# Eight blocks of the second layer's modulation move from the first layer's output projection into the scan's plan

## The chip, the cores and the metric

The kernel runs on one core of one Trainium2 chip. The metric is the device time of one execution in microseconds (us). Engines are named as in the profile: PE (TensorE, with PEld for its weight loads), DVE (VectorE), ACT (ScalarE), POOL (GpSimd) and SP (SyncE, which here mostly issues DMAs).

## The reference

Two layers work on 512 latent tokens and 256 context tokens of width 1024. The first layer's mixer is a gated MLP with spatial mixing, the second's a bidirectional RWKV-7 scan; each is followed by a mixture of experts. Every layer is modulated by vectors made from the conditioning:

```python
for i in range(DEPTH):
    mod_l = silu_c @ ada_w[i] + ada_b[i]
    mod_c = silu_cc @ ada_w[i] + ada_b[i]
    sh1, sc1, gt1, sh2, sc2, gt2 = jnp.split(mod_l[:, None, :], N_MOD, axis=-1)
    csh1, csc1, cgt1, csh2, csc2, cgt2 = jnp.split(mod_c, N_MOD, axis=-1)
    hl = rmsnorm(x, norm1_g[i]) * (1 + sc1) + sh1
    ...                                   # mixer of the layer, on hl and hc
    x = x + gt1 * yl
    hl2 = rmsnorm(x, norm2_g[i]) * (1 + sc2) + sh2
    ...                                   # experts on hl2
    x = x + gt2 * hier_moe(...)
```

`ada_w[i]` is 1024 x 6144 floats, 24 MB a layer. The second layer's mixer needs only the first third of its product (`sh1`, `sc1`); `gt1` is wanted after the scan, and the rest by the experts behind it.

## The kernel before

**Modulation.** The 6144 columns of a layer are made in 12 blocks of 512. `ada_block` loads a block's 2 MB of weights in four DMAs of 512 KB into the ring `w_raw`, and `ada_product` multiplies: eight matmuls with the conditioning as the stationary operand (128 x 32, in four column tiles of the array, so that four partial sums stand in four groups of partitions), a copy of the 128 x 512 result to `ada_part` by ACT, four small matmuls with `sel` that add the groups and turn the row into columns (the "turn"), and an addition of the bias by DVE into `k.mod[l]`. Product and turn share one PSUM buffer (tag `ada`, one deep).

**Where the blocks stand.** The first layer's blocks are spread over the first layer's mixer (`phase_a`): 0 to 3 ahead of it, 4 to 7 and 8 to 11 between its two projections' column groups. The second layer's twelve stand in the output projection at the end of `phase_a`: for each half `n` of the columns a loop over `kb` takes two rows of weights (`load_split`, split into a high and a low part) and makes 36 matmuls of 512 columns; in rounds 0 to 5 of each half a block is made with it. `moe.load_early` then issues the first expert weights.

**The scan's plan.** After the first layer's experts, `Rwkv.run` projects and then runs the scan (`wkv`). The scan's order is made by a planner (`Plan`): every step has an engine, an assumed cost, its reads and writes, and a tag; buffers come from rings of fixed depth (`RINGS`). `Plan.run` takes, again and again, the step that can start first by these costs, and among the steps of its engine that could start within `WINDOW` (0.05 us) the one whose tag number plus `DUE` is lowest:

```python
t0, s0 = min(best, key=lambda x: x[0])
t, s = min((x for x in best if x[1].eng == s0.eng and x[0] <= t0 + WINDOW), key=lambda x: x[1].tag[1] + DUE[x[1].tag[0]][x[1].tag[2]])
```

The steps: `value` (the value projection, 48 PE steps of six matmuls, tag 0, due +8), `prep` of group m (attention within a chunk, tag 2m, due -3 or -5), `invert` of group m (tag 2m, due -0.5; a chain of 62 DVE operations with transposes and two pairs of PE products), and `scan` step h (tag h, due 0). There are six groups of four chunks (two directions, two chunks each). `late` releases the memory of the value projection and makes the state `S` and the buffers of the second set; it reads all stores of `value`, and all steps with such a buffer come behind it. `Plan.fill` puts filler matmuls (L1061) ahead of a PE step that is the first user of a PSUM bank: at least one for the rings `p` and `y`, more where the plan sees PE idle for over 0.3 us. `p` has three banks. `QY` holds a chunk's masked products from `prep` until the scan step of that chunk has read them. The instructions are then ordered once more by the compiler.

Of the kernel before, what the change touches and what calls it, by code (L numbers as in the profile page):

```python
# [9 lines left out]
F32 = mybir.dt.float32  # L10
# [3 lines left out]
ALU = mybir.AluOpType  # L14
# [3 lines left out]
P = 128  # L18
# [84 lines left out]
def ada_block(k, pool, ps, l, n, bufs=4, tag="ada", psbufs=1):  # L103

    ws = []
    for h in range(4):
        w = pool.tile([P, 2, 512], F32, name="w_raw", tag="w_raw", bufs=bufs)
        k.nc.sync.dma_start(w, ada_rows(k, l, n, 2 * h, 2))
        ws += [w[:, i, :] for i in range(2)]
    ada_product(k, ps, pool.tile([P, 512], F32, name="ada_part", bufs=1), l, n, ws, tag, psbufs)  # L110


def ada_rows(k, l, n, j, m):
# [4 lines left out]
def ada_product(k, ps, part, l, n, ws, tag="ada", bufs=1):  # L118
    nc = k.nc
    q = ps.tile([P, 512], F32, name="ada_ps", tag=tag, bufs=bufs)  # L120
    for j, w in enumerate(ws):
        g = j % 4
        nc.tensor.matmul(q[32 * g:32 * g + 32, :], k.cstat[:, j, :], w, start=(j < 4), stop=(j >= 4),  # L123
                         tile_position=(0, 32 * g))
    nc.scalar.copy(part, q)
    q2 = ps.tile([P, 8], F32, name="ada_ps2", tag=tag, bufs=bufs)
    for j in range(4):
        nc.tensor.matmul(q2[:, 2 * j:2 * j + 2], part[:, j * P:(j + 1) * P], k.sel, start=True, stop=True)
    b = k.pk("adab")[:, l * 48 + 4 * n:l * 48 + 4 * n + 4]
    nc.vector.tensor_tensor(k.mod[l][:, 4 * n:4 * n + 4, :], q2.rearrange("p (j s) -> p j s", s=2),  # L130
                            b[:, :, None].to_broadcast([P, 4, 2]), op=ALU.add)


def mod(k, l, which, s):
# [46 lines left out]
def phase_a(k, moe):  # L181
    nc, tc = k.nc, k.tc
    a = k.a
    with ExitStack() as es:
# [12 lines left out]
        rms_stats(k, sm, v[:, 2, D:], rstd, range(NT), "r1")  # L197
        for n in range(4):
            ada_block(k, wp, ps, 0, n)
        G1 = gains(k, sm, 0, 1, k.pk("n1g")[:, 0:8], "G1")  # L200

        def emit_h(j, ql, qc):
# [36 lines left out]
        with tc.tile_pool(name="a_u", bufs=1) as up:  # L239
            for n in range(4):  # L240
# [13 lines left out]
                for i in range(4):  # L254
# [15 lines left out]
                    for hf in range(2):  # L270
# [7 lines left out]
                        nc.vector.tensor_tensor(v[:, 3 * hf:3 * hf + 3, g * P:(g + 1) * P], t1,  # L278
                                                u.rearrange("p (c q) -> p c q", c=3), op=ALU.mult)
                ada_block(k, wp, ps, 0, 8 + n)  # L280
        es_h.close()
        k.G2 = {0: gains(k, k.consts, 0, 4, k.pk("n2g")[:, 0:8], "G20")}

# [11 lines left out]
        for n in range(2):  # L295
            cs = slice(n * 512, (n + 1) * 512)
            acc = [ps.tile([P, 512], F32, name="o_ps", tag="mm") for t in range(NT)]
            for kb in range(KW // 2):
                ws = load_split(k, wp, a["ga_w_out"][kb * 256:(kb + 1) * 256, cs], 2)
                if kb < 6:  # L300
                    ada_block(k, wp, ps, 1, 6 * n + kb)
                gs = []
                for j in range(2):
                    g = 2 * kb + j
                    gh = og.tile([P, NT, P], F32R, name="gh", bufs=3)
                    gl = og.tile([P, NT, P], F32R, name="gl", bufs=3)
                    split(k, gh, gl, v[:, :, g * P:(g + 1) * P])
                    gs.append((gh, gl))

                for t, j in by_tile(NT, range(2), kb == KW // 2 - 1):  # L310
                    mm3(k, acc[t], (gs[j][0][:, t, :], gs[j][1][:, t, :]), ws[j], kb + j == 0, 2 * kb + j == KW - 1)
            for t in range(NT):
                tmp = og.tile([P, 512], F32, name="o_tmp", bufs=3)
                nc.vector.tensor_tensor(tmp, acc[t], gtB[t // NTL][:, cs], op=ALU.mult)
                nc.vector.tensor_tensor(k.x[:, t, cs], k.x[:, t, cs], tmp, op=ALU.add)
                moe.squares(og, t, n)
        moe.load_early()


# [4 lines left out]
class Moe:  # L324
# [570 lines left out]
    def overflow(self, ep, ps, after):  # L895
# [5 lines left out]
        with tc.For_i(0, nv) as i:  # L901
# [57 lines left out]
            for g in after.groups:  # L959
# [14 lines left out]
NCL = NL // C  # L974
DECAY = -0.6065306597126334
RINGS = dict(p=3, s3=2, sn=1, y=2, cum=1, kk=1, T=1, r=1, BK=1, set0=4, set1=4, X=1, Lp=1, Dn=1, subt=2, subp=2, SV0=1, SV1=1, rhs=1,
             yt=1, y0=1, E30=1, E31=1, fin=1, QY=8, v=4, vraw=2, vhi=4, vlo=4, vst=4)
SAME = dict(PE=0.1, DVE=0.13, ACT=0.15, POOL=0.1, SP=0.1)
WINDOW = 0.05
ON = dict(dec="POOL", q0="DVE", q1="DVE", r="POOL", neg="ACT", f1="POOL", f2="POOL", f3="DVE", f4="DVE")  # L980
COST = dict(DVE=0.6, POOL=1.32, ACT=0.48)
DUE = dict(prep=(-3.0, -3.0, -5.0, -5.0), invert=(-0.5, -0.5), scan=(0.0, 0.0), finish=(0.5,), value=(8.0,), late=(-9.0,))
PINNED = ()
DMALAT = 1.8
LAT = dict(PE=0.2, DVE=0.1, ACT=0.1, POOL=0.2, SP=0.2)
# [129 lines left out]
class Rwkv:  # L1115
# [6 lines left out]
    def run(self, moe):  # L1122
        k = self.k
        tc = k.tc
        k.G2[1] = gains(k, k.consts, 1, 4, k.pk("n2g")[:, 8:16], "G21")
        with ExitStack() as es:
            dr = es.enter_context(tc.tile_pool(name="c_dram", bufs=1, space=bass.MemoryType.DRAM))
            self.dr = dr
# [344 lines left out]
    def wkv(self, moe):  # L1473
# [4 lines left out]
        with ExitStack() as es:  # L1478
# [34 lines left out]
            prep(0, 0, 1, 2, 3)  # L1513
            self.invert(0)
            prep(1, 0, 1)
            for m in range(G):
                if m + 1 < G:
                    prep(m + 1, 2, 3)
                    self.invert(m + 1)
                for z in range(2):  # L1520
                    self.scan_step(2 * m, z, order[z][2 * m])
                if m + 2 < G:
                    prep(m + 2, 0, 1)
                for z in range(2):
                    self.scan_step(2 * m + 1, z, order[z][2 * m + 1])
            pl.run(tc)
            self.ps["y"].release()
            self.sp.release()
            self.out(moe)

    def values(self, vp):

# [637 lines left out]
```

## Time and profile before

| | us |
|---|---|
| median of 3 runs (lowest, highest) | 2725.82 (2725.16, 2739.96) |
| the profiled execution | 2729.52 |
| its span, from first to last instruction | 2727.3 |
| PE busy / DVE busy / ACT busy / POOL busy | 2430.3 / 1126.4 / 747.9 / 419.0 |
| mean granted clock of TensorE | 0.935 of full |

In the rows, `out<-in` names the tiles, `x` a count, and a bracket at a line's end is the idle time before the instruction and what ended it. A float32 matmul is recorded as two instructions; a busy PE is not a PE at its peak.

### The profile page before, as it was taken

The numbers are of one execution on the slowest core, as the hardware profiler recorded it, in microseconds if no ns is written. First come the engines' busy times: TensorE is split into PE (matmuls) and PEld (weight loads), VectorE is DVE, ScalarE is ACT, GpSimd is POOL, SyncE is SP. The second block draws the span as 40 slices with busy tenths as digits, with TensorE's granted clock in tenths as the row PEclk, the third lists the DMA queues.
The fourth block names the chain that finished last, engine by engine and source line by source line (L and its number), as shares of the span: only waits on it lengthen the run. The fifth ranks groups of instructions, "written<-read, shape, count | busy, mean of one in ns | idle before, by whom it ended". The sixth has DMA issues, their size and how long they took to land. (4 is left out here: it accounts for less than half of the span.)

```text
span 2727.3 us, 39031 instructions
## 1 busy us (share of the span) xinstructions
PE 2430.3 (89%) x15492; PEld 1533.4 (56%) x15492; DVE 1126.4 (41%) x2000; ACT 747.9 (27%) x1265; POOL 419.0 (15%) x339
## 2 busy tenths in 40 slices
PE   6999999976999999968979899889888599998994
PEld 2778996753443333336745488788777443333331
DVE  3335333374131111158654364887787611111113
ACT  3222123331000000026554346566543110000001
POOL 0000000033333322220012111112222301000001
PEclk8999999987999999988978699899989799999997
DMA  7136227565899999942245564434246569999994
GB/s 241 55 123 211 83 93 238 184 244 190 316 402 422 420 398 412 405 184 71 98 144 176 148 178 120 103 90 107 68 118 214 203 258 413 419 419 415 417 415 176
DMA packets 280943, 640.26 MB, mean 235 GB/s; under 512 B 131948, under 2 KB 157804, under 8 KB 230325
## 3 DMA queue, kind: packets, MB, share of 16 engines
q1 hardware_dynamic: 266548, 608.69, 60.9%
q0 software_dynamic: 12768, 23.78, 2.4%
q10 hardware_dynamic: 1440, 5.24, 0.5%
q8 instruction: 124, 2.03, 0.3%
q14 instruction: 63, 0.51, 0.1%
HBM read 582.22 MB, written 77.59 MB: 242 GB/s over the span
## 5 line engine op out<-in xcount | busy, mean ns | idle before, releaser
L827 PE MATMUL gu_ps<-e_raw,xT 128*64 128x512 f32 (+1 forms) x2048 | 629.7, 597 | 15.0 <-DMA e_raw<-moe_w_up 11.9
L827 PEld LDWEIGHTS gu_ps<-e_raw,xT 128*64 128x64 f32 (+1 forms) x2048 | 227.4, 154 | 388.0 <-issue 335.8
L845 PE MATMUL o_ps<-e_raw,hT 128*64 128x512 f32 (+1 forms) x1024 | 317.9, 601 | 5.0 <-ACT hT L792 5.0
L892 DVE TENSOR_TENSOR h_e<-gu_ps,h_e 128x512 f32<-128x512 f32 x42 | 29.1, 692 | 512.2 <-PE gu_ps L827 512.2
L845 PEld LDWEIGHTS o_ps<-e_raw,hT 128*64 128x64 f32 (+1 forms) x1024 | 114.5, 153 | 168.7 <-issue 150.2
L891 ACT ACTIVATE h_e<-gu_ps 128x512 f32<-128x512 f32 x42 | 25.1, 597 | 550.2 <-PE gu_ps L827 546.9
L1061 PE MATMUL p<-ident 128*128 128x128 f32 x892 | 140.4, 301 | 9.6 <-ACT BKt L1746 5.2
L1061 PEld LDWEIGHTS p<-ident 128*128 128x128 f32 x892 | 118.5, 204 | 22.2 <-ACT BKt L1746 7.2
L756 POOL DMA_INDIRECT ybuf<-yo,idx x40 | 40.0, 1001 | 472.3 <-DVE yo L848 403.3
L792 ACT COPY xT<-eT_ps 128x512 f32<-128x512 f32 x42 | 24.6, 585 | 321.0 <-PE gu_ps L827 205.5
L848 DVE SCALAR_TENSOR_TENSOR yo<-o_ps,wslot,gt_e 128x512 f32<-128x512 f32 x44 | 33.0, 750 | 184.8 <-issue 132.6
L749 POOL DMA_INDIRECT xg<-hbuf,idx x42 | 43.9, 1045 | 347.6 <-PE eT_ps L791 333.7
L73 PE MATMUL u_ps<-hh,w_hi 128*128 128x384 f32 x256 | 89.9, 351 | 5.0 <-ACT w_hi L66 5.0
L848 DVE SCALAR_TENSOR_TENSOR yo<-o_ps,wslot,gt2B 128x512 f32<-128x512 f32 x40 | 29.9, 750 | 155.0 <-PE o_ps L845 153.5
L74 PE MATMUL u_ps<-hl,w_hi 128*128 128x384 f32 x256 | 87.0, 340 | 0.0
L75 PE MATMUL u_ps<-hh,w_lo 128*128 128x384 f32 x256 | 85.9, 340 | 0.9 <-DVE w_lo L67 0.9
L67 DVE TENSOR_TENSOR w_lo<-w_raw,w_hi 128x1024 fp32r<-128x1024 f32 x56 | 67.9, 1222 | 38.4 <-ACT w_hi L66 37.9
L123 PE MATMUL ada_ps<-w_raw,cstat 128*32 128x512 f32 x384 | 64.0, 636 | 21.4 <-DMA w_raw<-ada_w 20.8
L73 PE MATMUL v_ps<-w_hi,hh 128*128 128x512 f32 x192 | 74.8, 402 | 4.2 <-ACT w_hi L66 4.2
L1776 DVE TENSOR_TENSOR X<-X,subt 128x31 f32<-128x31 f32 (+15 forms) x186 | 75.8, 408 | 5.0
L74 PE MATMUL o_ps<-w_lo,gh 128*128 128x512 f32 x192 | 76.1, 396 | 0.0
L73 PE MATMUL o_ps<-w_hi,gh 128*128 128x512 f32 x192 | 75.8, 398 | 0.0
(526 smaller groups left out, 4505.0 us busy)
## 6 DMA issues: line engine op xcount, KB each, us to landing
e_raw<-moe_w_gate SPq DMA_DIRECT2D x128, 1024.0 KB, 20.0
e_raw<-moe_w_up SPq DMA_DIRECT2D x128, 1024.0 KB, 20.2
e_raw<-moe_w_down SPq DMA_DIRECT2D x128, 1024.0 KB, 20.1
w_raw<-ada_w SPq DMA_DIRECT2D x96, 512.0 KB, 5.6
w_raw<-ga_w_in SPq DMA_DIRECT2D x32, 512.0 KB, 4.2
Td<-c_st SPq DMA_DIRECT2D x64, 192.0 KB, 3.3
T<-Td SPq DMA_DIRECT2D x24, 512.0 KB, 4.5
ybuf<-zero_rows SPq DMA_DIRECT2D x20, 512.0 KB, 7.1
```

The source lines that it names most:

```text
L67: k.nc.vector.tensor_tensor(lo, src, hi.bitcast(F32), op=ALU.subtract)
L73: mm(out, a[0], b[0], start=start, stop=False)
L74: mm(out, a[0], b[1], start=False, stop=False)
L75: mm(out, a[1], b[0], start=False, stop=stop)
L123: nc.tensor.matmul(q[32 * g:32 * g + 32, :], k.cstat[:, j, :], w, start=(j < 4), stop=(j >= 4), tile_position=(0, 32 * g))
L749: k.nc.gpsimd.indirect_dma_start(out=xg[:], out_offset=None, in_=self.hbuf[:, :], in_offset=bass.IndirectOffsetOnAxis(ap=self.idx[:, 1, b: ...
L756: st = self.k.nc.gpsimd.indirect_dma_start(out=self.ybuf[:, :], out_offset=bass.IndirectOffsetOnAxis(ap=self.idx[:, 0, b:b + 1], axis=0), ...
L827: mm(q[gu][rows], xT[i][:, kk, rows], self.raw[r, 2 * gu + kk // 4][:, f], start=kk == 0, stop=kk == KD - 1)
L845: mm(o[hf][rows], hT[i - 1][:, c, rows], self.raw[r, 4 + c // 2][:, f], start=c == 0, stop=c == 3)
L848: stt(yo[:, f], o[hf], self.wslot[:, u:u + 1], g[:, f], op0=ALU.mult, op1=ALU.mult)
L1061: nc.tensor.matmul(q[:, 0:128], self.ident, self.ident, start=True, stop=True)
L1776: eng.tensor_tensor(x, x, t.t.rearrange("p (a b) -> p a b", a=31 - j), op=ALU.subtract)
```

## The change

Three things. The turn of a block is no longer issued with its product but kept as a function (`k.ada_left`) and issued ahead of the next block's product, or by `ada_turn` at the end of a group of blocks. In the output projection only blocks 0 to 3 of the second layer remain (rounds 1 and 4 of each half). Blocks 4 to 11 become 32 pieces of 128 columns in the scan's plan (`modulation`): two loads of 256 KB each into the new ring `adaw` (two deep), two groups of four matmuls, one ACT copy, one turn, one DVE addition, with a bank of ring `p`. The pieces' tag is 1 + 10 i/32 and their due number 1. `QY` goes from eight buffers to seven, and the gains `G2[1]` are made after the plan.

```diff
--- before.py
+++ after.py
@@ -107,7 +107,15 @@
         w = pool.tile([P, 2, 512], F32, name="w_raw", tag="w_raw", bufs=bufs)
         k.nc.sync.dma_start(w, ada_rows(k, l, n, 2 * h, 2))
         ws += [w[:, i, :] for i in range(2)]
-    ada_product(k, ps, pool.tile([P, 512], F32, name="ada_part", bufs=1), l, n, ws, tag, psbufs)
+    ada_turn(k)
+    k.ada_left = ada_product(k, ps, pool.tile([P, 512], F32, name="ada_part", bufs=1), l, n, ws, tag, psbufs)
+
+
+def ada_turn(k):
+
+    left, k.ada_left = getattr(k, "ada_left", None), None
+    if left:
+        left()
 
 
 def ada_rows(k, l, n, j, m):
@@ -123,12 +131,16 @@
         nc.tensor.matmul(q[32 * g:32 * g + 32, :], k.cstat[:, j, :], w, start=(j < 4), stop=(j >= 4),
                          tile_position=(0, 32 * g))
     nc.scalar.copy(part, q)
-    q2 = ps.tile([P, 8], F32, name="ada_ps2", tag=tag, bufs=bufs)
-    for j in range(4):
-        nc.tensor.matmul(q2[:, 2 * j:2 * j + 2], part[:, j * P:(j + 1) * P], k.sel, start=True, stop=True)
-    b = k.pk("adab")[:, l * 48 + 4 * n:l * 48 + 4 * n + 4]
-    nc.vector.tensor_tensor(k.mod[l][:, 4 * n:4 * n + 4, :], q2.rearrange("p (j s) -> p j s", s=2),
-                            b[:, :, None].to_broadcast([P, 4, 2]), op=ALU.add)
+
+    def turn():
+        q2 = ps.tile([P, 8], F32, name="ada_ps2", tag=tag, bufs=bufs)
+        for j in range(4):
+            nc.tensor.matmul(q2[:, 2 * j:2 * j + 2], part[:, j * P:(j + 1) * P], k.sel, start=True, stop=True)
+        b = k.pk("adab")[:, l * 48 + 4 * n:l * 48 + 4 * n + 4]
+        nc.vector.tensor_tensor(k.mod[l][:, 4 * n:4 * n + 4, :], q2.rearrange("p (j s) -> p j s", s=2),
+                                b[:, :, None].to_broadcast([P, 4, 2]), op=ALU.add)
+
+    return turn
 
 
 def mod(k, l, which, s):
@@ -197,6 +209,7 @@
         rms_stats(k, sm, v[:, 2, D:], rstd, range(NT), "r1")
         for n in range(4):
             ada_block(k, wp, ps, 0, n)
+        ada_turn(k)
         G1 = gains(k, sm, 0, 1, k.pk("n1g")[:, 0:8], "G1")
 
         def emit_h(j, ql, qc):
@@ -278,6 +291,7 @@
                         nc.vector.tensor_tensor(v[:, 3 * hf:3 * hf + 3, g * P:(g + 1) * P], t1,
                                                 u.rearrange("p (c q) -> p c q", c=3), op=ALU.mult)
                 ada_block(k, wp, ps, 0, 8 + n)
+        ada_turn(k)
         es_h.close()
         k.G2 = {0: gains(k, k.consts, 0, 4, k.pk("n2g")[:, 0:8], "G20")}
 
@@ -297,8 +311,8 @@
             acc = [ps.tile([P, 512], F32, name="o_ps", tag="mm") for t in range(NT)]
             for kb in range(KW // 2):
                 ws = load_split(k, wp, a["ga_w_out"][kb * 256:(kb + 1) * 256, cs], 2)
-                if kb < 6:
-                    ada_block(k, wp, ps, 1, 6 * n + kb)
+                if kb in (1, 4):
+                    ada_block(k, wp, ps, 1, 2 * n + kb // 4)
                 gs = []
                 for j in range(2):
                     g = 2 * kb + j
@@ -314,6 +328,7 @@
                 nc.vector.tensor_tensor(tmp, acc[t], gtB[t // NTL][:, cs], op=ALU.mult)
                 nc.vector.tensor_tensor(k.x[:, t, cs], k.x[:, t, cs], tmp, op=ALU.add)
                 moe.squares(og, t, n)
+            ada_turn(k)
         moe.load_early()
 
 
@@ -974,12 +989,12 @@
 NCL = NL // C
 DECAY = -0.6065306597126334
 RINGS = dict(p=3, s3=2, sn=1, y=2, cum=1, kk=1, T=1, r=1, BK=1, set0=4, set1=4, X=1, Lp=1, Dn=1, subt=2, subp=2, SV0=1, SV1=1, rhs=1,
-             yt=1, y0=1, E30=1, E31=1, fin=1, QY=8, v=4, vraw=2, vhi=4, vlo=4, vst=4)
+             yt=1, y0=1, E30=1, E31=1, fin=1, QY=7, v=4, vraw=2, vhi=4, vlo=4, vst=4, adaw=2, adap=1)
 SAME = dict(PE=0.1, DVE=0.13, ACT=0.15, POOL=0.1, SP=0.1)
 WINDOW = 0.05
 ON = dict(dec="POOL", q0="DVE", q1="DVE", r="POOL", neg="ACT", f1="POOL", f2="POOL", f3="DVE", f4="DVE")
 COST = dict(DVE=0.6, POOL=1.32, ACT=0.48)
-DUE = dict(prep=(-3.0, -3.0, -5.0, -5.0), invert=(-0.5, -0.5), scan=(0.0, 0.0), finish=(0.5,), value=(8.0,), late=(-9.0,))
+DUE = dict(prep=(-3.0, -3.0, -5.0, -5.0), invert=(-0.5, -0.5), scan=(0.0, 0.0), finish=(0.5,), value=(8.0,), late=(-9.0,), ada=(1.0,))
 PINNED = ()
 DMALAT = 1.8
 LAT = dict(PE=0.2, DVE=0.1, ACT=0.1, POOL=0.2, SP=0.2)
@@ -1122,7 +1137,6 @@
     def run(self, moe):
         k = self.k
         tc = k.tc
-        k.G2[1] = gains(k, k.consts, 1, 4, k.pk("n2g")[:, 8:16], "G21")
         with ExitStack() as es:
             dr = es.enter_context(tc.tile_pool(name="c_dram", bufs=1, space=bass.MemoryType.DRAM))
             self.dr = dr
@@ -1513,6 +1527,8 @@
             prep(0, 0, 1, 2, 3)
             self.invert(0)
             prep(1, 0, 1)
+            for i in range(32):
+                self.modulation(i)
             for m in range(G):
                 if m + 1 < G:
                     prep(m + 1, 2, 3)
@@ -1526,7 +1542,30 @@
             pl.run(tc)
             self.ps["y"].release()
             self.sp.release()
+            k.G2[1] = gains(k, k.consts, 1, 4, k.pk("n2g")[:, 8:16], "G21")
             self.out(moe)
+
+    def modulation(self, i):
+
+        k, add = self.k, self.plan.add
+        nc = k.nc
+        self.plan.tag = "ada", 1 + 10.0 * i / 32, 0
+        part, q = self.buf("adap", [P, P], 1, RINGS["adap"]), self.bank([P, 4, P])
+        b = 16 + i
+        for h in range(2):
+            w = self.buf("adaw", [P, 4, P], 1, RINGS["adaw"])
+            self.load(0.73, lambda w=w: w.t, w, k.a["ada_w"][1, h * 512:(h + 1) * 512, b * P:(b + 1) * P].rearrange("(k p) f -> p k f", p=P))
+
+            def product(w=w, h=h):
+                for g in range(4):
+                    nc.tensor.matmul(q.t[32 * g:32 * g + 32, 0, :], k.cstat[:, 4 * h + g, :], w.t[:, g, :], start=(h == 0), stop=(h == 1),
+                                     tile_position=(0, 32 * g))
+
+            add("PE", 0.5, product, r=[w], w=[q])
+        add("ACT", 0.25, lambda: nc.scalar.copy(part.t, q.t[:, 0, :]), r=[q], w=[part])
+        add("PE", 0.3, lambda: nc.tensor.matmul(q.t[:, 1, 0:2], part.t, k.sel, start=True, stop=True), r=[part], w=[(q, "turned")])
+        add("DVE", 0.17, lambda: nc.vector.tensor_tensor(k.mod[1][:, b, :], q.t[:, 1, 0:2], k.pk("adab")[:, 48 + b:49 + b].to_broadcast([P, 2]),
+                                                         op=ALU.add), r=[(q, "turned")])
 
     def values(self, vp):
 
```

## Rows read from the trace of the kernel before

**Rows 1.** The page's 40 slices: DMA share in tenths

```profile
DMA  7136227565899999942245564434246569999994
```

**Rows 2.** Windows: start:end, us, busy us (x instructions) by engine, PEclk, DMA share, GB/s

```profile
420.00:440.00 20.00, 20.00 (x112) 13.99 (x111) 4.56 (x8) 5.78 (x7) 0.00 (x0) 1.00 0.60 195
...
1554.00:1656.00 102.00, 100.59 (x762) 82.91 (x763) 56.06 (x104) 46.38 (x88) 15.65 (x18) 0.93 0.58 166
...
1720.00:1775.00 55.00, 51.36 (x744) 47.13 (x743) 45.91 (x106) 28.35 (x58) 5.79 (x8) 0.93 0.39 84
```

**Rows 3.** Timeline of PE in the projection: start us, us, engine, line, operation

```profile
422.47 1.92 PE L123 MATMUL ada_ps<-w_raw,cstat 128*32 128x512 f32 x16
...
430.17 0.39 PE L73 MATMUL o_ps<-w_hi,gh 128*128 128x512 f32 x1
...
433.34 0.39 PE L75 MATMUL o_ps<-w_hi,gl 128*128 128x512 f32 x1
433.66 1.92 PE L123 MATMUL ada_ps<-w_raw,cstat 128*32 128x512 f32 x16
```

**Rows 4.** Timeline of SP's DMA issues at the projection's end

```profile
552.39 0.88 SPq L172 DMA_DIRECT2D w_raw<-ga_w_out  x2
553.32 0.94 SPq L439 DMA_DIRECT2D e_raw<-moe_w_gate  x2
```

**Rows 5.** PE's groups by line, 1554 to 1656: busy us, mean ns, idle before

```profile
L74 PE MATMUL v<-vlo,xh 128*128 128x512 f32 x96 | 39.9, 416 | 0.0
L73 PE MATMUL v<-vhi,xh 128*128 128x512 f32 x96 | 39.8, 420 | 0.9 <-ACT vhi L66 0.9
L75 PE MATMUL v<-vhi,xl 128*128 128x512 f32 x96 | 39.7, 414 | 0.0
...
L1061 PE MATMUL p<-ident 128*128 128x128 f32 x58 | 10.8, 296 | 0.5 <-ACT BKt L1746 0.4
```

**Rows 6.** Timeline of PE, POOL and DVE, around the value part and the scan

```profile
1554.09 2.08 PE L73 MATMUL v<-vhi,xh 128*128 128x512 f32 x4 [0.94 <-ACT vhi L66]
...
1655.78 0.40 PE L75 MATMUL v<-vhi,xl 128*128 128x512 f32 x1
...
1660.97 0.98 POOL L1579 DMA_INDIRECT vd<-vst,rev  x1 [3.29 <-DMA vd<-vst,rev]
1661.94 1.01 POOL L1618 MEMSET S<- 128x512 f32 x2
...
1671.56 0.48 PE L1858 MATMUL s<-SV,ZZ 128*64 128x64 f32 x2
...
2064.28 0.68 DVE L1912 TENSOR_TENSOR S<-sn,S 128x512 f32<-128x512 f32 x1
```

**Rows 7.** PE's waits, 0 to 400: us in total, times, longest

```profile
PE ada_ps L123 <- DMA w_raw<-ada_w: 19.9, 6, 14.1
...
PE ada_ps L128 <- ACT ada_part L125: 4.5, 7, 0.8
```

**Rows 8.** Timeline of PE: a filler and what follows it

```profile
1574.29 0.49 PE L1061 MATMUL p<-ident 128*128 128x128 f32 x2
1574.62 0.60 PE L1743 MATMUL p<-ident,BK 128*128 128x128 f32 x4
```

**Rows 9.** The modulation's instructions: duration ns min/median/max, first and last start

```profile
L123 PEld LDWEIGHTS ada_ps<-w_raw,cstat x384: 106/109/155, 14.0 to 552.2; 128*32 128x32 f32 x192
...
L128 PE MATMUL ada_ps<-sel,ada_part x192: 165/251/272, 20.2 to 554.9; 128*128 128x2 f32 x192
...
L130 DVE TENSOR_TENSOR mod<-ada_ps,packed x24: 166/167/167, 21.3 to 555.2; 128x8 f32<-128x8 f32 x24
```

**Rows 10.** DMA issues, 1554 to 1610 and 1610 to 1660: KB each, median us to landing

```profile
kk<-kkd SPq DMA_DIRECT2D x5, 256.0 KB, 5.0
...
vd<-vst SPq DMA_DIRECT2D x10, 256.0 KB, 2.7
```

**Rows 11.** Timeline of DVE and PE around the fourth inversion

```profile
1825.58 1.94 DVE L1767 STREAM_TRANSPOSE Lp<-XT 128x1024 f32<-128x1024 f32 x1 [0.32 <-ACT XT L1731]
...
1841.18 2.04 PE L1878 MATMUL y<-SV,QY 128*64 128x64 f32 x64
...
1864.78 2.00 DVE L1798 STREAM_TRANSPOSE Lp<-X 128x1024 f32<-128x1024 f32 x1
...
1883.90 1.20 PE L1811 MATMUL p<-Dn,XT 32*32 32x32 f32 x64
```

## The prediction

> **What bounds the kernel now.** I read the page's 40 slices first [rows 1]: DMA is at nine tenths in slices 12 to 17 and 34 to 39, the two expert stages, and hardly anywhere else. The change touches neither of these but two stages ahead of them, so I read those two by windows [rows 2]. The reader should see that they have different limits. In the output projection of the first layer (window 420 to 440) PE is busy 20.00 of 20 us at a granted clock of 1.00 (the 2.4 GHz level), while DVE has 4.56 and ACT 5.78: PE bounds it, and whatever leaves PE there is gained. In the scan's first part (1554 to 1656) PE is busy 100.59 of 102 us, again the full engine. In the later scan (1720 to 1775) DVE has 45.91 of 55 us; there the scan goes by DVE and by waits on PSUM banks.
>
> The third view is the PE timeline of the projection [rows 3]: one round of `kb` lasts from the first modulation product at 422.47 to the next at 433.66. The fourth is the PE work of 1554 to 1656 by lines [rows 5] and the timeline around its end [rows 6]. There the reader should see a chain: the last value matmul at 1655.78, POOL's last scattered store at 1660.97, the memset of the state at 1661.94 (it belongs to `late`, which waits for all stores of `value`), the first scan matmul at 1671.56. So the end of `value` on PE sets the start of the scan, with 15.8 us behind it.
>
> **Part 1, blocks taken out of the projection.** A round is 433.66 - 422.47 = 11.19 us [rows 3]. Its 36 projection matmuls (six token tiles, two rows of weights, three products) go at (433.34 - 430.17)/14 = 0.2264 us each, 8.15 us. A modulation block therefore costs 3.04 us of a full PE, its eight products, turn and changes of operand together. Eight of twelve leave: 24.3 us. The very first block partly fills a wait for weights; if it gave nothing the sum would be 21.3. I take 24. The shorter round still has cover: DVE's 4.56 and ACT's 5.78 of 20 us [rows 2] are far from the bound. The gain is passed on, since the first expert loads stand behind the last projection load on SP (552.39, then 553.32 [rows 4]) and move with it.
>
> **Part 2, the deferred turn.** Nothing is removed: the same four small matmuls, one ACT copy and one DVE addition per block, and the block's PSUM buffer is still single, so the next product still waits for the addition. In the first 400 us PE waited 4.5 us in all for the copy [rows 7], most of it while it had to wait for weights anyway. Bounds -4.5 and, if each of some 20 blocks waited once more for a DVE addition of 0.17 us [rows 9], +3.4; I take 0, because the matmuls between are there in both orders.
>
> **Part 3, the 32 pieces in the scan: where they land.** The planner gives an engine to the step that can start first, and among steps within 0.05 us to the one with the lowest due number (`run` of `Plan`). A piece i has 1 + 10 i/32 + 1, a value step has 8, preparation has -3 and -5, inversion -0.5. So pieces 0 to 19 (2.0 to 7.9) go ahead of value steps wherever both can start. Their two loads depend on nothing but the ring `adaw`, and are ready from the start. By the planner's own steps (load 0.73 and 1.8 latency, product 0.5, value step 1.3) a piece comes round every 3.9 us or so: 20 of them in 78 us, inside the value part. They are called "1 to 11" but are not spread over the scan: a due number orders ties, it holds nothing back. These figures give the order only; the time is from rows.
>
> **What a piece costs on PE.** It issues eight 128x32 products of 128 columns, one turn, and one filler of 128x128, since it is the first user of a bank of ring `p`. Filler: 1574.62 - 1574.29 = 0.33 us [rows 8]. Turn: two records of 165 to 251 ns that can overlap [rows 9], 0.2 to 0.5. Products from both sides: a quarter of the 512-column block, (3.04 less about 0.9 for its turn)/4, is 0.5; if the 16 weight loads of 109 ns [rows 9] stood in a row it would be 1.7. So a piece lies between 1.0 and 2.5 us; I take 1.4, nearer the lower end, because four column tiles run side by side in the trace's own blocks. Twenty pieces are 28 us (20 to 50).
>
> **What covers it.** Little. In 1554 to 1656 the value matmuls alone are 288 records [rows 5] at 0.2264, 65 us; idle time is 1.4 us and fillers are 10.8 us, of which the 20 that a bank's first use always takes are 20 x 0.33 = 6.6. So some 4 us can be reused, and 28 - 4 = 24 us push the end of `value`, and with it the scan, the second inversion and the rest.
>
> **Their loads.** A product stands in PE's order; if its load is late, the value matmuls behind it wait too. Per round the slot is free for about 3.6 us of other PE work. A 256 KB load landed in 5.0 us (median) before 1610 and in 2.7 us after [rows 10], and its issue comes on top: late by some 2 us in the first half, not in the second. For about ten pieces that is 0 to 20 us; I take 8, because late loads also leave the preparation time to get ahead. The pieces' issues cost SP some 0.44 us each (two in 0.88 [rows 4]), 18 us for the first forty; SP's other loads and stores queue behind an `adaw` load that waits for its slot, which is counted here. The ACT copies (twenty, under 0.6 us each) find ACT at 46.38 of 102 us [rows 2]. By the Trainium skill, "DMA: Bandwidth & Descriptors", section "Anatomy of one DMA", a DMA takes about 2.0 us plus its bytes at 436 GB/s, which makes 2.6 us for 256 KB; the quiet half agrees (2.7 us), the busy half does not (5.0 us), and by the page alone this term would be 0 and the sum 8 us lower.
>
> **The other twelve pieces** fall right behind, where preparation and inversion of the second group stand on the chain with DVE at 45.91 of 55. PE is hidden there (fillers give way). DVE gets twelve additions of 0.17 us, 2 us, and each piece holds one of the three `p` banks. 0 to 15; I take 5.
>
> **Part 4, seven QY buffers for eight.** The last chunk of group 3 can now be prepared only when a step of scan 4 has read its QY. Before, that group's inversion began at 1825.58, while scan 4's outputs ran at 1841.18 [rows 11]. With some 8 us for the attend and its copies, the inversion would begin near 1849, 24 us later. But its DVE part ended at 1866.8 and PE took its result only at 1883.90: 17 us of slack. So 7 at this place, 0 to 24, and twice more with less; a scan step can be pulled forward into the gap. I take 5 in all. Moving the two tiny DVE operations of `G2[1]` behind the plan costs under half a us.
>
> **Sum.** -24 + 0 + 24 + 8 + 5 + 5 = +18 us. The profiled execution took 2729.52 us (span 2727.3 and 2.2 around it), 3.7 above the median 2725.82. 2729.5 + 18 = 2747.5 on its scale, 2744 on the median's.
>
> **Rivals.**
> 1. The pieces hide after all: the compiler's final order, which already puts small matmuls between value matmuls, lets them run in the fillers behind the value part. For it: fillers are plentiful later in the scan. Against it: PE has no room before 1656, and the pieces stand ahead in the plan. Then -24 + 5 + 5 to -24 + 0: 2702 to 2712, faster by 0.5 to 0.9%. It decides against me if fewer than some ten pieces run before the last value matmul. The Trainium skill, "Perfetto Trace Analysis", section "Optimization Strategy", says that interleaving stretches whose most contended engines differ can help; by that rule the time is this rival's. The trace bears it out only where DVE is the limit, not in the first 102 us of the plan.
> 2. Late loads and banks: products wait 20 us in the busy half, the weight loads stand in a row (2 us a piece), QY costs its 24. -24 + 36 + 20 + 10 + 15 = +57: 2783. For it: the DMA landing of 5.0 us. Against it: the second half is quiet.
> 3. The reordered plan happens to shorten the scan as well, because its chain was not the tightest one: -24 and another 10 or more, 2690. Nothing in the rows speaks for it but that the order changes as a whole.
>
> **How the numbers follow.** The forecast, slower by a few us to 40, gets 0.45, rival 1 0.28, rival 2 0.20, rival 3 0.07. About 1% (27 us) is what a measurement can tell. Time 2744. The range holds rival 1's lower end and rival 2's bound: 2700 to 2785; the forecast's own range is 2728 to 2766. Faster by over 1%: rival 3's larger part, 0.05. Slower by over 1% (above 2753): a third of the forecast's chance (0.15) and most of rival 2, 0.33. Same: 0.62.
>
> **What would show it.** The projection's round 8.15 us without a block, and the first expert load some 24 us earlier. Between the start of `value` and its last matmul, about 20 pieces; the stretch from the first value matmul to the memset of the state (now 1554.09 to 1661.94 [rows 6]) longer by 25 to 40 us; PE waits on `adaw` loads in its first half. The stretch from that memset to the last state update (2064.28 [rows 6], now 402 us) nearly unchanged or up to 15 longer. I am wrong if pieces run mostly behind `value`, if a piece takes under 0.8 us of PE, or if the stretch behind the memset moves by more than 15 us.

## The result, and the profile after

The changed kernel took 2770.39 us (median of 4 runs, 2766.47 to 2782.42) against 2728.22 (4 runs beside it): ratio 1.0154, 95% interval 1.011 to 1.0198. It is slower, by more than the 1% that I had called measurable. The profiled execution has a span of 2770.3 us, 43.0 more than before.

A table by stages carries the rest of this document. It is worked out from single rows of each run's timeline: the first `ga_w_out` load and the first `e_raw` load on SP, the first value matmul on PE, POOL's memset of the state, the start of DVE's last state update, and the span. The time ahead of the first load (400.7 to 409.7 us) has no column. "adaw" is the number of load buffers for the pieces, "bank" whether pieces use the ring `p` or a bank of their own.

| run | pieces in the scan | QY | adaw | bank | projection | to first value matmul | value part | scan behind the memset | rest | span |
|---|---|---|---|---|---|---|---|---|---|---|
| before | 0 | 8 | - | - | 152.6 | 1000.8 | 107.9 | 402.3 | 663.0 | 2727.3 |
| after | 32 | 7 | 2 | p | 120.1 | 1001.5 | 106.0 | 473.3 | 666.0 | 2770.3 |
| before_qy7 | 0 | 7 | - | - | 153.7 | 1000.4 | 106.5 | 431.8 | 662.6 | 2759.7 |
| qy8_adaw1 | 32 | 8 | 1 | p | 120.1 | 1003.0 | 106.2 | 428.6 | 676.6 | 2738.7 |
| turn_only | 0 | 8 | - | - | 153.8 | 1005.9 | 106.7 | 404.8 | 663.7 | 2736.8 |
| proj_mod | 0 | 8 | - | - | 120.1 | 1115.3 | 106.4 | 404.8 | 664.6 | 2816.3 |
| value16 | 0 (16 in value) | 8 | 2 | p | 134.1 | 1006.2 | 125.4 | 408.7 | 663.7 | 2747.7 |
| nofill | 32 | 8 | 1 | p | 120.1 | 996.8 | 103.7 | 449.6 | 681.7 | 2756.2 |
| ownbank | 32 | 8 | 1 | own | 120.1 | 1003.4 | 106.1 | 416.1 | 671.9 | 2723.6 |
| route8 | 0 | 8 | - | - | 123.2 | 1037.0 | 106.6 | 404.5 | 663.8 | 2739.7 |
| after_ownbank | 32 | 7 | 2 | own | 120.1 | 998.0 | 103.7 | 459.1 | 662.0 | 2749.5 |
| before_y1 | 0 | 8 | - | - | 152.8 | 1004.9 | 108.0 | 404.2 | 659.6 | 2736.3 |
| mix | 16 | 8 | 1 | own | 120.1 | 1015.1 | 106.3 | 403.1 | 663.2 | 2712.9 |
| mix24 | 24 | 8 | 1 | own | 120.1 | 1008.3 | 104.9 | 400.7 | 665.1 | 2703.0 |

Stages whose code is the same differ between runs by a few us (the unchanged scan: 402.3 to 404.8; the stretch to the first value matmul: 997 to 1006), so a difference under 5 us in one of them is not read as an effect. Each row is one execution, and the executions of a kernel differ: those in the table took 6 to 10 us less than the median of their kernel for nofill, ownbank, mix, qy8_adaw1 and mix24, 5 us more for before_y1 and 13 more for turn_only. No trace shows where the other executions spent the difference, so whole kernels are compared by their medians.

The timeline of the changed kernel at the ends of its stages (start us, us, engine, line, operation) answers to [rows 4, 6]:

```profile
522.05 1.39 SPq L184 DMA_DIRECT2D w_raw<-ga_w_out  x3
523.49 0.97 SPq L454 DMA_DIRECT2D e_raw<-moe_w_gate  x2
...
1524.98 1.65 PE L73 MATMUL v<-vhi,xh 128*128 128x512 f32 x3 [0.94 <-ACT vhi L66]
...
1630.98 1.01 POOL L1657 MEMSET S<- 128x512 f32 x2
...
2104.30 0.68 DVE L1951 TENSOR_TENSOR S<-sn,S 128x512 f32<-128x512 f32 x1
```

The first expert load is 29.8 us earlier (523.49 for 553.32), the first value matmul 29.1, the memset 31.0. Then it turns: the last state update, 402 us behind the memset before, is 473 behind it now. -31.0 + 71.0 + 3.0 (rest) is the whole +43.

The pieces' load buffers, in the view of one tile (instructions, what they waited for, who waited):

```profile
L1561 PE MATMUL p<-adaw,cstat x512: 272/297/423, 1648.1 to 1995.5; 128*32 128x128 f32 x171
L1682 SPq DMA_DIRECT2D adaw<-ada_w x64: 367/374/1320, 1635.2 to 1990.4; - x64
...
  DMA adaw<-ada_w: 13.1, 14
...
DMA to landing us min/median/max: 2.5/2.9/3.9
```

The first of 64 loads is issued at 1635.2, behind the memset at 1630.98. No piece ran in the value part. `buf` takes the pool as its third argument; the 1 in `self.buf("adaw", [P, 4, P], 1, ...)` puts the buffer into the pool that opens with `late`, so that every piece waits for `late`. I had read that 1 as a count.

The scan by windows (start:end, us, busy by engine, PEclk, DMA share, GB/s), of before and of after:

```profile
1662.00:2064.00 402.00, 360.21 (x6290) 322.66 (x6290) 311.67 (x638) 234.63 (x463) 83.56 (x93) 0.93 0.43 105
```

```profile
1631.00:2104.00 473.00, 411.66 (x6837) 358.00 (x6835) 311.22 (x675) 244.72 (x496) 80.81 (x93) 0.86 0.49 125
```

DVE has the same 311 us of work in both. What was added is small: by lines, in the stretch 1640 to 2000, the products are 27.6 us of PE (0.86 a piece) and the turns 13.3:

```profile
L1561 PE MATMUL p<-adaw,cstat 128*32 128x128 f32 x512 | 27.6, 318 | 5.7 <-DMA adaw<-ada_w 5.6
...
L1566 PE MATMUL p<-sel,adap 128*128 128x2 f32 x62 | 13.3, 284 | 6.9 <-ACT adap L1565 6.9
```

So 71 us came with some 41 us of matmuls. PE's busy time is 51 us longer, its idle time 20 (42 of 402 us before, 61 of 473 after). Fillers count as busy, so these rows alone do not tell whether the work itself or its order and waits lengthened the scan; the runs below are there for that.

One more row of the changed scan matters. Ahead of the 32 small additions that end the pieces, DVE stands idle for 63.4 us:

```profile
L1567 DVE TENSOR_TENSOR mod<-p,packed 128x2 f32<-128x2 f32 x32 | 4.8, 150 | 63.4 <-PE p L1566 50.6 <-ACT rhs L1928 12.6
```

In the scans of the runs below it is 21.6 us (qy8_adaw1), 19.9 (ownbank), 48.6 (after_ownbank) and 9.9 (mix24). Idle time is not yet delay, and no run moves the additions alone, so how much of the scan's growth is theirs stays open.

### The profile page after: what moved, and what is told of

Read it like the earlier page. It is cut to its first block, busy times and chain, and to the rows that moved or that the text cites. A ratio compares the mean times of both kernels' runs of the same rounds, so it can differ in the third digit from the quotient of the medians.

```text
span 2770.3 us, 39814 instructions
## 1 busy us (share of the span) xinstructions
PE 2451.7 (88%) x15836; PEld 1554.2 (56%) x15836; DVE 1123.6 (41%) x2024; ACT 752.7 (27%) x1289; POOL 416.2 (15%) x339
## 4 chain that ended last, share of the span: by engine, by line
PE 45%; DMA 13%; DVE 13%; ACT 3%; issue 2%; POOL 1%; SPq 1%; DVEq 0%; ACTq 0%; POOLq 0%
PE gu_ps L842 16%; PE o_ps L860 8%; DMA e_raw<-moe_w_down 4%; DMA e_raw<-moe_w_gate 4%; DMA e_raw<-moe_w_up 3%; PE p L1076 3%; PE eT_ps L806 2%; DVE subt L1810 2%; DVE X L1815 1%; PE p L1761 1%; PE g_ps L1467 1%; PE p_ps L73 1%; PE p_ps L74 1%; PE p_ps L75 1%; DVE xm L1196 1%
## 5 line engine op out<-in xcount | busy, mean ns | idle before, releaser
L842 PE MATMUL gu_ps<-e_raw,xT 128*64 128x512 f32 (+1 forms) x2048 | 629.8, 598 | 15.1 <-DMA e_raw<-moe_w_up 11.9
L1076 PE MATMUL p<-ident 128*128 128x128 f32 x874 | 154.9, 316 | 23.2 <-ACT BKt L1785 8.0
L906 ACT ACTIVATE h_e<-gu_ps 128x512 f32<-128x512 f32 x42 | 25.1, 597 | 550.7 <-PE gu_ps L842 546.8
L1076 PEld LDWEIGHTS p<-ident 128*128 128x128 f32 x874 | 125.6, 214 | 40.9 <-issue 11.3
L75 PE MATMUL v_ps<-w_hi,hl 128*128 128x512 f32 x192 | 75.7, 394 | 0.0
L74 PE MATMUL v_ps<-w_lo,hh 128*128 128x512 f32 x192 | 75.4, 394 | 0.0
L75 PE MATMUL o_ps<-w_hi,gl 128*128 128x512 f32 x192 | 74.9, 390 | 0.0
```

Of the source, the lines that this page charges most:

```text
L74: mm(out, a[0], b[1], start=False, stop=False)
L75: mm(out, a[1], b[0], start=False, stop=stop)
L842: mm(q[gu][rows], xT[i][:, kk, rows], self.raw[r, 2 * gu + kk // 4][:, f], start=kk == 0, stop=kk == KD - 1)
L1076: nc.tensor.matmul(q[:, 0:128], self.ident, self.ident, start=True, stop=True)
```

## Experiments

**One buffer of QY less, nothing else (before_qy7).**

```diff
-             ... fin=1, QY=8, v=4, ...
+             ... fin=1, QY=7, v=4, ...
```

> The kernel before with one edit: the ring QY has seven buffers for eight; no piece is in the plan, all twelve blocks stay in the projection. In the kernel after, the stretch from the memset of the state to the last state update is 473.3 us (before: 402.3). Theory A, the lost QY buffer does it: the stretch grows to 450 to 470 us, in steps of some 20 us at scan steps 6, 8 and 10, and the time to 2775 to 2795. Theory B, the pieces do it (their time on PE, their hold on the banks of ring p, their place in SP's queue): the stretch stays within 402 to 410 and the time within 2725 to 2735.

Measured 2760.47 us, ratio 1.0099 (1.0067 to 1.0131); all of it in the scan, +29.5. The direction is theory A's, the size is less than it expected. PE's busy time in the scan grew too, from 360.6 to 389.4 us, though no work was added: the fillers in the ring `p` went from 115.5 to 141.5. DVE's timeline around the fourth inversion:

```profile
1819.81 1.38 DVE L1693 TENSOR_TENSOR ZZ<-kk,E 64x512 f32<-64x512 f32 x2
1838.20 2.28 DVE L1693 TENSOR_TENSOR ZZ<-kk,E 64x512 f32<-64x512 f32 x2 [17.01 <-PE y L1875]
...
1853.65 0.42 DVE L1736 TENSOR_TENSOR QY<-p,maskY 128x256 f32<-128x256 f32 x1 [0.77 <-ACT XT L1731]
1853.99 2.00 DVE L1767 STREAM_TRANSPOSE Lp<-XT 128x1024 f32<-128x1024 f32 x1
```

DVE, otherwise the busiest engine here beside PE, stands idle 17.01 us (the trace names a scan step's output matmul as what released it); then the last chunk's QY is written and the inversion begins. The starts of the inversions behind the memset:

| | 2nd | 3rd | 4th | 5th | 6th |
|---|---|---|---|---|---|
| before | 39.5 | 101.5 | 163.6 | 238.4 | 310.6 |
| before_qy7 | 39.3 | 100.9 | 188.7 | 264.0 | 342.0 |
| after | 50.5 | 117.6 | 212.0 | 297.2 | 383.5 |

The fourth is 25.1 us late. Scan step 6, which uses it, starts its update only 3.5 later; but step 8 is 13 and step 10 is 33 us late. I read this as a slack that was there once and then used up. The Trainium skill, "Perfetto Trace Analysis", section "Optimization Strategy", says that a gap that repeats on the engine which should be busy can mean that there is no room for the next tile. The trace agrees: the 17.01 us of DVE come back as 10.15 us ahead of the same line at 1913.07.

**The pieces without that loss (qy8_adaw1).** Two load buffers and eight QY do not fit together, so the pieces have one load buffer.

```diff
-             ... QY=7, ... adaw=2, adap=1)
+             ... QY=8, ... adaw=1, adap=1)
```

> The kernel after with eight QY buffers again; to make room the ring adaw is one deep for two, so the pieces come more slowly. Theory A: the stretch from the memset to the last state update is 405 to 420 us and the time 2700 to 2715, since the 30 us of the projection stay. Theory B: the stretch stays at 460 us or more and the time at 2760 or more.

2750.61 us, ratio 1.0067 (1.0044 to 1.0089); the scan of 428.6 us lies between the two theories. It is 26.3 longer than before, and the rest 13.6: with one load buffer only 27 of the 32 pieces are finished at the last state update, the last addition comes 41.6 us behind it, and `G2[1]` needs it. So the scan alone does not compare like with like (29.5 + 26.3 for the 71.0 of the change). Scan and rest taken together, the lost buffer costs 29.1 us, the pieces 39.9, and both 74.0. That is 5 more than their sum and not read as an effect: in these executions the two add.

**The deferred turn alone (turn_only).** Twelve blocks in the projection, `ada_turn` as in the change.

```diff
-    ada_product(k, ps, ...)
+    ada_turn(k)
+    k.ada_left = ada_product(k, ps, ...)
```

> Only the deferred turn: all twelve blocks of the second layer stay in the projection, no piece in the plan, eight QY buffers. Up to the first expert load the kernel after gained 29.8 us where the prediction took 24. Theory A (the deferral is worth nothing, the rounds without a block gain more than the 3.04 us): 2726 to 2731, the first expert load at 553. Theory B (the deferral owns the rest): that load at 547 and the time 2720 to 2723.

2726.03 us, ratio 0.9985 (0.9962 to 1.0008): nothing that can be seen, as the sum had it.

**The blocks in the second layer's `project` (proj_mod).** Eight whole blocks there, each with its turn at once.

Against the changed kernel, with QY 8:

```diff
+                for n in range(8):
+                    low.insert(9 + 5 * n, lambda n=n: block(4 + n))
...
-            for i in range(32):
-                self.modulation(i)
```

> The eight blocks are made neither in the output projection nor in the plan, but in the second layer's projections ahead of the scan, one block after every fourth decay step, from eight loads of 256 KB each; eight QY buffers, the plan as before. If PE is covered there (it is busy 39.8 of 40 us at 1320 to 1360 but 19.6 of 40 at 1200 to 1240, with DVE at 33.4): the time is 2700 to 2710. If each block costs its 3 us of PE and waits for its loads: 2725 to 2745. By theories A and B alike the scan's stretch is that of before, 402 us.

2817.34 us, ratio 1.0296, far outside both expected ranges: the stretch to the first value matmul is 114 us longer. DVE by lines, 1240 to 1430:

```profile
L1392 DVE TENSOR_TENSOR mod<-lr_ps,packed 128x8 f32<-128x8 f32 x8 | 1.3, 167 | 104.7 <-PE lr_ps L1390 104.7
```

Eight additions of 167 ns; DVE stood idle 104.7 us ahead of them, 13 each on average. The block's products wait for loads and are spread between other matmuls, the addition stands in DVE's order, and the decay's work on DVE stands behind it. I take the place of the addition for the cause, but this run does not show it by itself: the blocks also take buffers of the decay's staging ring `l_st` and of its PSUM ring `lr_ps`.

**Pieces where I had thought them (value16).** 16 pieces with buffers from the value part's own pool, eight blocks in the projection, QY 8, `vst` 3.

```diff
+            for i in range(16, 32):
+                self.modulation(i, vp)
+                keys.append(("ada", i))
             self.plan.tag = "late", 0, 0
...
-            w = self.buf("adaw", [P, 4, P], 1, RINGS["adaw"])
+            w = Buf("adaw", lambda: vp.tile([P, 4, P], F32, name="adaw", tag="adaw", bufs=RINGS["adaw"]))
```

> What the recorded prediction meant by a piece inside the value part, built so that it happens: blocks 8 to 11 as 16 pieces whose buffers come from the pool that is open in the value part (the store ring `vst` 3 instead of 4 makes room), `late` behind them, the other eight blocks in the projection, QY 8. Theory of the prediction (the part is bound by PE, a piece adds its own 1.2 us): the value part 107.9 + 16 x 1.2 = 127 us, the projection 12 us shorter, the scan as before at 402 to 405: about 2737. Rival (pieces hide behind the value matmuls): the value part stays at 106 to 109, about 2718.

2746.92 us, ratio 1.0055 (1.0037 to 1.0074). The value part is 125.4 us for 107.9: 17.5 / 16 = 1.09 us a piece. The scan is 6.4 us longer too, though no piece was planned into it, and the time is 10 above the 2737 expected; why is not known. PE's window of the value part, up to its last value matmul:

```profile
1550.00:1664.00 114.00, 112.48 (x1000) 85.27 (x1001) 56.80 (x116) 49.59 (x100) 14.56 (x18) 0.99 0.75 211
```

PE is busy 112.48 of 114 us: the part is bound by PE. By PE's rows 13 of the 16 pieces stand ahead of the last value matmul, which comes 12.3 us later after the first than before, 0.94 a piece; the other three come behind it, around the memset. The pieces did not hide in this place; at 1.09 us, four pieces cost 4.4, more than the 3.3 that a block gives back in the projection (below).

**No filler ahead of a piece (nofill).**

```diff
-        if s.eng != "PE":
+        if s.eng != "PE" or s.tag[0] == "ada":
             return
```

> The run with QY 8 and one `adaw` buffer, but with no filler matmul put ahead of a piece's first product. Theory P (what lengthens the scan by 26 us is TensorE's time for the pieces and for the fillers that come with them): the scan loses a filler of about 0.3 to 0.6 us 32 times, so 10 to 19 us: 410 to 419 us behind the memset. Theory K (it is the `p` bank that a piece keeps from its first product to its addition): the scan stays at 425 to 432 us, total 2747 to 2754.

2764.41 us, ratio 1.012 (1.0079 to 1.0161); the scan 449.6 us, 21 longer than with the fillers. Both theories missed. PE's waits in that scan:

```profile
PE p L1561 <- DMA adaw<-ada_w: 18.6, 15, 2.7
```

Waits for `adaw` are 18.6 us for 6.3 with the fillers, which stood ahead of the product and ran while its load was under way; that is 12 of the 21. The others stay open, and there is a rival: without these fillers PE's granted clock in the scan was 0.84 for 0.90, and its busy time rose from 376.6 to 384.0 us. The run does speak against theory P: with fewer matmuls on PE the scan became longer, not shorter.

**A PSUM bank of their own (ownbank), and its control (before_y1).** The ring `y` gives one of its two banks; no fillers there.

```diff
-RINGS = dict(p=3, s3=2, sn=1, y=2, ...
+RINGS = dict(pa=1, p=3, s3=2, sn=1, y=1, ...
...
-self.bank([P, 4, P])
+self.bank([P, 4, P], "pa")
```

> The run with QY 8 and one `adaw` buffer, but the pieces have a PSUM bank of their own (taken from the ring `y`, 1 instead of 2); that ring gets no fillers either. Theory K (the `p` banks that the pieces hold): the scan falls back to 402 to 412 us, so about 2730 to 2737 with the end of the pieces still behind the scan. Theory P (TensorE's time): the same as the run without the pieces' fillers, whatever that gives. If the second `y` bank mattered, both fall and the scan is over 430.

> Control: the kernel before with the ring `y` at 1 instead of 2, nothing else. If the second `y` bank is spare, the scan stays at 400 to 406 us and the total at 2726 to 2734; if it is not, the scan grows, and by so much the pieces with a bank of their own were charged too much (416 us behind the memset in that run).

ownbank: 2732.56 us, ratio 0.999 (0.997 to 1.001), the scan 416.1, 4 above theory K's range. before_y1: 2732.71, ratio 1.0004 (0.9986 to 1.0021), the scan 404.2, so the bank of `y` was spare. Against qy8_adaw1 the scan is 12.5 us shorter, against nofill, which has no fillers at the pieces either, 33.5. PE's lines of the fillers in the ring `p`, first of qy8_adaw1, then of ownbank:

```profile
L1076 PE MATMUL p<-ident 128*128 128x128 f32 x504 | 103.1, 333 | 27.1 <-ACT BKt L1785 9.9 <-DVE QY L1775 7.0 <-ACT XT L1770 6.7
```

```profile
L1076 PE MATMUL p<-ident 128*128 128x128 f32 x374 | 75.1, 323 | 13.3 <-ACT BKt L1785 7.0 <-DVE QY L1775 3.2 <-ACT XT L1770 1.6
```

A filler is the first user of a bank, so the idle time ahead of fillers is mostly a wait for a bank: 27.1 us with the pieces in the ring, 13.3 with their own, 9.1 in the scan before. The steps behind it in PE's order wait too. The 13.8 us between the first two are about the 12.5 that the scan gained.

**The changed kernel with that bank (after_ownbank).** The same edit on the changed kernel.

> The changed kernel with one edit: its pieces have a bank of their own (the ring `y` 1 instead of 2, no fillers in the pieces' bank). What the bank was worth with QY 7: if the lost buffer of QY (+29.5 us) and the pieces' banks (+26, of which the own bank gave back 12.5) add, the scan is 402 + 29.5 + 14 = 446 us, the total about 2743. If the two only make each other worse through the `p` banks (the 15 us by which 71 is more than 29.5 + 26.3), the scan is 432 to 440. If the bank has nothing to do with it here, 465 to 475, about 2770.

2753.76 us, ratio 1.0081 (1.005 to 1.0113); the scan 459.1, 14.2 less than in the change and in none of the three ranges. The bank is worth about the same with QY 7 as with QY 8. Against ownbank the scan is 43.0 us longer, but ownbank also has one load buffer for two and leaves four pieces behind its scan. Scan and rest together, the difference is 33.1, close to the 29.1 that the lost QY buffer costs without pieces. QY 7 with one load buffer and pieces was not run.

**The blocks in the first layer's routing (route8).** Blocks 4 to 11 where PE waits between the last projection matmul and the first expert's; two expert weights fewer are loaded ahead, to make room.

```diff
+        if l == 0:
+            for b in [4, 5]:
+                ada_block(k, rp, ps, 1, b, 4, "hT", 6)
...
-RAW = (3, 7, 3), (5, 6, 5)
+RAW = (3, 5, 5), (5, 6, 5)
```

> The kernel before with blocks 4 to 11 of the second layer made neither in the projection nor in the scan, but in the first layer's routing, where TensorE stands idle about 40 us between 594.9 and 644.9 us of the run before: two behind the logits' products, two behind the counts, four behind the table. RAW[0] is (3, 5, 5) instead of (3, 7, 3), so two expert weights fewer are loaded ahead and 16 KB are free for the blocks' loads. Theory S (the projection gives 24 us back and the idle time takes the products, 8 x 3 us): the stretch from the last expert load of the projection to the first value matmul stays at 1000 to 1005, 2702 to 2710. Rival (16.8 MB of loads stand on the same queue ahead of the first experts' weights, and the stage behind it is bound by loads): up to 16.8 MB / 0.42 MB per us = 40 us later, 2720 to 2745.

2742.2 us, ratio 1.0045 (1.0015 to 1.0075). From the routing's first transpose to the first expert matmul it took 655.79 - 560.85 = 94.9 us, for 646.72 - 578.74 = 68.0 before. The timeline of PE shows the last blocks between the table and the first expert:

```profile
621.33 1.26 PE L678 MATMUL tab<-rows,hot 128*128 128x44 f32 x5
...
645.65 5.21 PE L123 MATMUL ada_ps<-w_raw,cstat 128*32 128x512 f32 x16 [0.26 <-DMA w_raw<-ada_w]
...
655.79 4.56 PE L836 MATMUL gu_ps<-e_raw,xT 128*128 128x512 f32 x10
```

The gap holds some blocks, not eight. Four stand behind the table, and from 621 to 656 PE is busy 29.33 of 35 us at a granted clock of 0.73; its waits for `w_raw` are only 4.3 us in the whole gap. So it is mostly these products, ahead of the first expert in PE's order, that fill the 26.9 us.

**Mixed versions (mix, mix24).** Own bank, QY 8; blocks 0 to 3 in the projection. mix: 4 to 7 in the routing, 8 to 11 as 16 pieces. mix24: 4 and 5 in the routing, 6 to 11 as 24 pieces. Against ownbank (mix24; mix has `range(16, 32)`):

```diff
-            for i in range(32):
+            for i in range(8, 32):
                 self.modulation(i)
```

> A version meant to beat both. The run with a bank of their own for the pieces, but only blocks 8 to 11 (16 pieces) in the scan; blocks 4 to 7 in the first layer's routing (one ahead of the logits' last products, two behind them, one behind the counts, RAW[0] = (3, 5, 5)), blocks 0 to 3 in the projection. If pieces with their own bank cost the scan only what TensorE has free: projection 120 us as in the other runs with four blocks there (-32), routing 4 to 10 us longer, scan 402 to 410 (+0 to +8), nothing behind the scan, since 16 pieces end well before it: 2702 to 2725. Rival (the half of what lengthened the two runs that it is put together from: routing +37/2, scan +14/2): 2722 to 2727. If the four blocks in the routing still push the first experts by as much as the eight did, about 2740.

> The mixed version with two blocks (7 pieces' worth of wait in the routing) moved on: blocks 4 and 5 in the first layer's routing (one ahead of the logits' last products, one behind them), blocks 6 to 11 as 24 pieces in the scan with a bank of their own, blocks 0 to 3 in the projection. 16 such pieces left the scan at 403.1 us, 32 made it 416.1 and the rest 8 us longer. If the pieces are free as long as they end before the scan does: projection 120, the stretch to the first value matmul 1003 to 1009 (half of the +14 of four blocks), scan 403 to 410, rest 663 to 666: 2702 to 2716. If the scan pays for each piece beyond 16 in proportion: scan 410, rest 667, 2714 to 2722, no better than the mixed version (2722.6).

mix: 2722.56 us, ratio 0.9971 (0.9953 to 0.9989). mix24: 2715.03 us, ratio 0.9944 (0.9921 to 0.9966), faster than both kernels, though by less than 1%. Its scan by windows:

```profile
1637.00:2038.00 401.00, 352.87 (x6302) 303.97 (x6301) 313.33 (x671) 239.17 (x483) 84.22 (x94) 0.88 0.52 132
```

With 24 pieces the scan takes 400.7 us, no longer than without any; 22 of them are finished in it, the last addition starts at 2055.86, 18 us behind the last state update, and the rest is as long as it was (665.1 for 663.0). PE is busy 352.87 us there, less than the 360.21 of before: the pieces took the place of fillers (79.4 us in the ring `p` for 115.5). By the medians mix24 gains 11.9 us, by the spans of the two executions 24.3, so the table is the more favourable view. 32 pieces in the same bank took 416.1. Why the last eight cost so much was not tried further; in that run the last piece's loads go out at 2086, behind the last state update at 2051.67. The two blocks in the routing cost at most 7.5 us by the table (1008.3 for 1000.8), little more than that stretch varies.

## Why the prediction was right in its range and wrong in its place

2770 lies inside the range 2700 to 2785, outside the forecast's own 2728 to 2766. The chances put "within 1%" first; slower by over 1%, which had 0.33, came. That the total is near is luck: two large errors of opposite sign. Two of the three signs named for being wrong came: the pieces run behind `value`, and the stretch behind the memset moved by 71 us.

- **Projection, -24.** Right and a little small. From the last matmul of the stage ahead (398.70 before, 401.35 after) to the last `o_ps` (578.50 and 554.91) in PE's timeline it is 179.8 and 153.6 us: -26.2, 3.3 us a block for my 3.04. The first value matmul gained 29.1; the 3 us between lie within what that stretch varies.
- **Deferred turn, 0.** Right (turn_only).
- **Where the pieces land.** The step that failed is the sentence "Their two loads depend on nothing but the ring `adaw`, and are ready from the start." They depend on `late`. The products start at 1648.1, behind the memset at 1630.98. The planner's order was worked out well from a wrong start. With it fell the terms +24 and +8: the value part was 106.0 us for 107.9.
- **What a piece costs on PE.** Right, where I had it: 24 us for 20 pieces is 1.2, value16 gave 0.94 to 1.09. In the scan it is 0.86 of products and 0.43 of turn, close to the 1.4 less a filler. It was only not what set the time there.
- **Their loads.** I took 5.0 us to land from the busy half of the value part; in the scan they took 2.9 (median of 64). The 2.7 us beside it were no load: that row is a store (`vd<-vst`). The Trainium skill, "DMA: Bandwidth & Descriptors", section "Anatomy of one DMA", has a fit for DMAs issued through GpSimd, from which 2.6 us for 256 KB is an estimate. These loads are issued by SP; their 2.9 us are nearer to it than my 5.0.
- **The other twelve pieces, +5.** I named the cause, one of three `p` banks for each piece, and mis-sized it. With QY 8, 32 pieces cost 26.3 us in the scan, of which the bank is 12.5, and 13.6 behind it. What is left went away with eight pieces fewer, as 24 in their own bank left scan and rest at 1065.8 us for 1065.3. DVE's idle time ahead of the pieces' additions is a rival that no run separates; I had counted only the additions themselves, 2 us for twelve.
- **Seven QY buffers, +5.** The delay of the inversion was computed rightly: "near 1849, 24 us later"; it came 25.1 later. What failed is the discount, "17 us of slack ... I take 5 in all". The slack was real at the fourth inversion (step 6 only 3.5 late), but the fifth and sixth are late by 25.6 and 31.4, and nothing pays that back. The term is 29.5 us alone and some 33 beside the pieces, scan and rest together. Together with the pieces it lengthened the scan by 71 us where I had 10; the 32 us that I had put into the value part and that never came made up for half of that, which is why the total is near.
- **The rivals.** Rival 1's condition (pieces behind the last value matmul) was met, its time (2702 to 2712) was not: in the change the fillers in the ring `p` did not give way (115.5 us before, 130.9 after), and banks and QY were short. The Trainium skill's rule that interleaving stretches with different contended engines can help ("Perfetto Trace Analysis", "Optimization Strategy") is not borne out by the change; mix24, with the same idea, fewer pieces and without the two borrowed buffers, comes to 2715. Rival 2 had nearly the time (2783), for reasons that were not the ones.

## What to carry to other kernels

Before placing moved work, look up what its buffers depend on: a pool that opens late is a start time, whatever the due numbers say. Work moved into an engine's spare time also borrows buffers, and these were the larger part of the price that the runs could name: a ring that turns once per period has its delay at every period, so a slack found once must not be taken off again at the next. Give moved work a bank that is spare and no more pieces than the stage can finish: 24 pieces, two of which ended just behind it, left this scan as long as it was.

## What the runs showed of the hardware that I had not expected

- A scan at a lower granted clock was no slower: a mean over its two levels (1.2 and 2.4 GHz) of 0.93 with 402.3 us in before, 0.88 with 400.7 in mix24. PE's work in the two is not the same (pieces took the place of fillers), so this is no price of the clock; it shows only that the clock told little about the length of this stage.
- Taking away matmuls that do nothing made a stage 21 us longer (nofill): by PE's waits, 12 us of it are loads that they had covered for the products behind them. The granted clock fell with them, from 0.90 to 0.84, and its share is open.
- Ahead of eight additions of 167 ns DVE stood idle 104.7 us (proj_mod), with the work behind them in its order waiting.
